# First projections in groups between the token transposes; decay and beta columns split in two parts and multiplied after the tokens; all token loads issued first

## The chip, the cores and the metric

The kernel runs on one core of one Trainium2 chip. The metric is device microseconds of one execution; lower is better. TensorE (PE) does the matrix work, with VectorE (DVE), ScalarE (ACT) and GpSimd (POOL) around it; SyncE (SP), ACT and POOL issue DMAs.

## The reference, cut to what matters

One inference step of a hybrid layer: a combined projection of 1024 prompt tokens and 8 sample tokens, dilated-window attention heads and gated-DeltaNet heads fed from it, an output projection, and a two-level mixture of experts. What the change touches is the start: the projection, the short convolution behind it, and the decay and beta of the DeltaNet heads.

```python
qa, ka, va, ub, zb, ab, bb = split_proj(hp @ w_in[l])
u_ext = jnp.pad(ub, ((0, 0), (CONV_WIDTH - 1, 0), (0, 0)))
q, k, v, g, beta = deltanet_features(short_conv(u_ext, conv_w[l], S), ab, bb, a_log[l], dt_bias[l])
# in deltanet_features:
g = -jnp.exp(a_log) * jax.nn.softplus(a_raw + dt_bias)
beta = jax.nn.sigmoid(b_raw)
# in gated_delta_chunked: gc = cumsum(g) per chunk, decay = exp(gc_i - gc_j),
# then a triangular solve and a scan over chunks
```

## The kernel before, in words

**Tokens.** The 1032 tokens (eight tiles of 128 and one of 8) are loaded as rows into `xt` (L306), odd tiles by SP's queue, even tiles by ACT's. Per tile PE transposes two halves of four 128x128 blocks into a PSUM tile `xps` (L311, pool `tp`, two buffers). DVE copies each half to SBUF as `xf` (L314), ACT rounds it to the high part `xh` (L315, a cast to fp32r), and POOL subtracts the two to get the low part `xl` (L316).

**Decay and beta columns.** The eight columns `wab` of w_in that give decay and beta are multiplied per tile in fp32 with `xf` (L321). The result `ab` holds four partial sums at 32-partition steps; nine matmuls with a selection matrix (L333) add and transpose it into `abt`. From `abt` a chain of small steps on DVE, ACT and PE makes `gdec` (L357), its running sums `gc` (L363, L366), and a transposed copy `gcr` (L379), which goes to DRAM and comes back broadcast as `gb` for each head. The sample tokens' part of `abt` makes a trip through DRAM (`ab_d`, `absm`, L336 to L338) first. `cwr`, the rows of the convolution weights (L386), shares `gcr`'s buffer, so it is loaded when `gcr` has been stored; PE transposes it and the conv state into `cp` (L391), and DVE copies `cw` (L394). No convolution can start before `cw`.

**Projections.** A weight is 128 columns of w_in. `weight` loads it into the single `raw` buffer (L251, SP's queue), ACT casts the high part (L254), DVE subtracts the low part (L255); two buffers `w` hold such pairs. `proj` runs three groups of 344 tokens; a group is 24 matmuls (L278 to L280) into one of two PSUM buffers, and ACT copies the group out. The DeltaNet inputs are called U(j,h) here: j is 0, 1, 2 for the two inputs of `kq` and for `vt`, h the head; their columns start at 1536 + (4j + h) x 128, so w1536 is U(0,0), w2048 U(1,0), w2176 U(1,1), w2688 U(2,1). Two buffers `U` hold a projected input; the next one's first write (a POOL memset, L297) waits for the convolution of the input two before it.

**A head.** DVE convolves (`acc`, L427 to L429, four operations of 1024), ACT takes tanh, DVE makes `kq` (L435); PE multiplies `kk` (L460); DVE applies the decay (`ft`, `qk`, L461, L462); then a substitution of many small DVE steps (`xm`, `xb`, L524 to L534) ends in `xy` (L537), and PE and DVE go on in turns from the `z` of L556. Projections of later inputs stand on PE between these steps.

**Order.** The body is written once; a scheduler sets each engine's order when the program is built, and that order is then fixed: every engine runs its own list from top to bottom, and an instruction whose wait isn't over holds all behind it. `after(later, earlier)` adds edges by hand. `FIRST` names the token tiles behind which the first two weights are split. A DMA waits, besides its data, for the DMA that last used its semaphore (the DMAHW names in the order).

Of the kernel before, what the change touches and what calls it, by code (L numbers as in the profile page):

```python
# [94 lines left out]
def _consts():  # L95
    i = np.arange(P)[:, None]
    j = np.arange(P)[None, :]
    c = [np.eye(P), (i < j), np.broadcast_to(j, (P, P)), i % 64 == np.arange(36)[None, :]]
    cm = np.concatenate([np.asarray(x, np.float32) for x in c], axis=1)

    c = [(i <= j), np.where(j >= i, 0.0, -BIG), i // 16 == j // 16]
    for s in LEVELS:
        c.append((i // (2 * s) == j // (2 * s)) & ((i // s) % 2 == 1) & ((j // s) % 2 == 0))
    c += [i % 16 == np.arange(16)[None, :], i % 32 == np.arange(8)[None, :]]
    cd = np.concatenate([np.asarray(x, np.float32) for x in c], axis=1)
    oh = np.concatenate([_bias_rows(1023 - np.arange(RT)), _bias_rows(DECD)], axis=1)
# [16 lines left out]
def body(ctx, tc, I, O, C):  # L123
    nc = tc.nc
# [8 lines left out]
    dram = pool(ctx, "dram", space=DRAM)  # L133

    cm = const.tile([P, C["c_mats"].shape[1]], F32, name="cm")
    nc.sync.dma_start(out=cm, in_=C["c_mats"])
    ident, strict, iota = (cm[:, n * P:(n + 1) * P] for n in range(3))
    sel36 = cm[:, 3 * P:3 * P + 36]
    ones = const.tile([P, P], F32, name="ones")
# [61 lines left out]
    phs = ExitStack()  # L201
    sm2 = pool(phs, "sm2", bufs=2)
    cd = sm2.tile([P, C["c_delta"].shape[1]], F32, name="cd", bufs=1)
    nc.gpsimd.dma_start(out=cd, in_=C["c_delta"])
    tri, maskb, m16 = (cd[:, n * P:(n + 1) * P] for n in range(3))
    lvl = {s: cd[:, (3 + n) * P:(4 + n) * P] for n, s in enumerate(LEVELS)}
    i16 = cd[:, (3 + len(LEVELS)) * P:][:, :16]
# [19 lines left out]
    def tiles(ap, n=P):  # L227

        return ap[:, 0:S].rearrange("p (a b) -> p a b", b=n)
# [53 lines left out]
            evac(g, ps)  # L283
            yield


    wab = sm2.tile([P, KD, 8], F32, tag="rows", name="wab", bufs=1)
    nc.sync.dma_start(out=wab, in_=I["w_in"][0, :, 3584:3592].rearrange("(k p) c -> p k c", p=P))
    ab = T4("qk", "ab")
    nc.gpsimd.memset(ab, 0.0)  # L290
    xraw, xhi, first = {}, {}, {}

    def conv_in(ct, groups):

# [4 lines left out]
        proj(1536 + ct * P, lambda g, ps: nc.scalar.copy(out=U[:, 3 + g * G:3 + (g + 1) * G], in_=ps), groups)  # L299
        return U  # L300

    for t in range(NT + 1):
        n = P if t < NT else NS
        xt = T4(("ktl", "vh", "zt", "ktl", "vh", "zt", "os", "gb", "ft")[t], f"xt{t}")
        src = I["x_prompt"][0, t * P:(t + 1) * P, :] if t < NT else I["x_sample"][:, 0, :]
        (nc.sync if t % 2 else nc.scalar).dma_start(out=xt[:n], in_=src)  # L306
        xf = tiles(T4(("acc", "vt")[t % 2], f"xf{t}"))
        for b in range(2):
            ps = tps(f"xps{t}_{b}")
            for k in range(4):  # L310
                nc.tensor.transpose(ps[:, k, :n], xt[:n, (4 * b + k) * P:(4 * b + k + 1) * P], ident[:n, :n])  # L311
            hi = xh[:, 4 * b:4 * b + 4, t * P:t * P + n]
            raw_ = xf[:, 4 * b:4 * b + 4, :n]
            xraw[t] = nc.vector.tensor_copy(out=raw_, in_=ps[:, :, :n])  # L314
            xhi[t] = nc.scalar.copy(out=hi, in_=ps[:, :, :n])  # L315
            nc.gpsimd.tensor_tensor(out=xl[:, 4 * b:4 * b + 4, t * P:t * P + n], in0=raw_, in1=hi.bitcast(F32), op=OP.subtract)  # L316
        if t % 4 == 0:
            pab = mm.tile([P, 4, P], F32, tag="mm", name=f"ab_{t}")
        for q in range(2):
            for c in range(4):  # L320
                nc.tensor.matmul(pab[32 * c:32 * c + 8, t % 4, :n], wab[:, 2 * c + q, :], xf[:, 2 * c + q, :n], start=(q == 0), stop=(q == 1))  # L321
        if t % 4 == 3 or t == NT:
            w = (t % 4) * P + n
            for c in range(4):
                r = slice(32 * c, 32 * c + 8)
                (nc.scalar.copy if c in ABA else nc.vector.tensor_copy)(out=ab[r, t // 4 * 512:t // 4 * 512 + w],
                                                                     in_=pab[r].rearrange("p a b -> p (a b)")[:, :w])
# [313 lines left out]
    def biases():  # L641

        rb = small.tile([33, NH], F32, name="rb")
        nc.gpsimd.memset(rb, 1.0)
        nc.gpsimd.dma_start(out=rb[:32], in_=I["rel_bias"])
        cb = T8("dtf", "cb")
        nc.gpsimd.dma_start(out=cb[:33, :RT + 225], in_=C["c_bias"])
        brow = T8("kq", "brow")
        w = RT // 3
        for b in range(3):  # L650
            ps = tps(f"bps{b}").rearrange("p a b -> p (a b)")
            nc.tensor.matmul(ps[:NH, :w], rb, cb[:33, b * w:(b + 1) * w], start=True, stop=True)
# [950 lines left out]
```

## Time and profile before

| | us |
|---|---|
| runs shown | 1529.11, 1530.95, 1539.24 |
| median | 1530.95 |
| profiled execution | 1527.0 |
| its span | 1525.2 |

The profiled execution's own time is 1.8 us above its span, and the median of the runs is 3.95 us above the profiled execution. All times of instructions in this text are of that execution and count from the start of its span. The first 132 us of the span are what the change touches; behind them the fixed orders of before and after are the same on every engine.

### The profile page before, as it was taken

What the parts mean: (1) busy time and instruction counts of PE and PEld (TensorE: products, weight loads), DVE (VectorE), ACT (ScalarE), POOL (GpSimd) and SP (SyncE); (2) the same over time, 40 slices, a digit from 0 to 9 for tenths busy, and PEclk for the clock granted to TensorE, in tenths of its full rate; (3) what the DMA queues carried; (4) which work ended last, traced back from release to release, by engine and by line L of the source; (5) the groups of instructions that cost most, each with busy time, mean ns of one, the idle gap of its engine ahead of it and who ended that gap; (6) DMA issues with size and microseconds to landing.
All of it is one profiled execution on the core that took longest, in us unless ns stands there. A gap on an engine that the chain in (4) does not pass through costs nothing. (4 is left out here: it accounts for less than half of the span.)

```text
span 1525.2 us, 22948 instructions
## 1 busy us (share of the span) xinstructions
PE 1414.8 (93%) x8084; PEld 1168.1 (77%) x8085; DVE 1101.5 (72%) x2105; ACT 881.0 (58%) x1754; POOL 357.4 (23%) x346
## 2 busy tenths in 40 slices
PE   5999999997999989999999969999999999999970
PEld 3989798886987868775767658888888888888850
DVE  4577786867444536356546669999999999999968
ACT  3333534343243424344321149999999999999964
POOL 7020313224022250112301221111112211111115
PEclk9999999999999999995999969999999999999995
DMA  5231110102332461245873569999999999999955
GB/s 173 95 125 29 44 42 24 49 15 75 91 113 84 118 159 55 71 109 174 232 248 132 195 244 349 351 374 372 360 354 352 353 368 368 354 358 367 348 167 222
DMA packets 140016, 309.39 MB, mean 203 GB/s; under 512 B 13483, under 2 KB 71775, under 8 KB 139888
## 3 DMA queue, kind: packets, MB, share of 16 engines
q1 hardware_dynamic: 113928, 259.21, 47.0%
q0 software_dynamic: 14720, 33.92, 8.8%
q10 hardware_dynamic: 11248, 14.75, 3.1%
q8 instruction: 65, 1.06, 0.3%
q14 instruction: 55, 0.45, 0.1%
HBM read 284.04 MB, written 45.24 MB: 216 GB/s over the span
## 5 line engine op out<-in xcount | busy, mean ns | idle before, releaser
L1353 DVE TENSOR_TENSOR wl<-p,wh 128x512 fp32r<-128x512 f32 x436 | 269.9, 682 | 1.1 <-ACT wh L1352 1.1
L1352 ACT CAST wh<-p 128x512 fp32r<-128x512 f32 x436 | 254.1, 633 | 18.3 <-PE h L1389 8.2
L278 PE MATMUL pp<-xh,w 128*128 128x344 f32 x672 | 227.8, 339 | 1.5 <-ACT w L254 1.5
L279 PE MATMUL pp<-xl,w 128*128 128x344 f32 x672 | 221.3, 329 | 0.0
L280 PE MATMUL pp<-xh,w 128*128 128x344 f32 x672 | 220.1, 328 | 0.4 <-DVE w L255 0.4
L1387 PE MATMUL h<-wh,eh 128*128 128x512 f32 x512 | 206.6, 404 | 0.0
L1388 PE MATMUL h<-wl,eh 128*128 128x512 f32 x512 | 205.4, 401 | 0.4 <-DVE wl L1353 0.4
L1389 PE MATMUL h<-wh,el 128*128 128x512 f32 x512 | 201.0, 393 | 0.0
L278 PEld LDWEIGHTS pp<-xh,w 128*128 128x128 f32 x672 | 127.7, 190 | 11.5 <-issue 7.0
L280 PEld LDWEIGHTS pp<-xh,w 128*128 128x128 f32 x672 | 128.0, 190 | 2.3 <-issue 1.2
L279 PEld LDWEIGHTS pp<-xl,w 128*128 128x128 f32 x672 | 128.0, 190 | 1.9 <-issue 1.5
L1359 POOL MEMSET xg<- 128x1024 f32 x32 | 30.5, 953 | 398.2 <-PE xp L1372 396.3
L1388 PEld LDWEIGHTS h<-wl,eh 128*128 128x128 f32 x512 | 96.6, 189 | 25.3 <-DVE wl L1353 7.8
L1353 DVE TENSOR_TENSOR wl_d<-p,wh_d 128x512 fp32r<-128x512 f32 x188 | 115.4, 680 | 0.0
L1352 ACT CAST wh_d<-p 128x512 fp32r<-128x512 f32 x188 | 109.4, 621 | 3.2
L1387 PEld LDWEIGHTS h<-wh,eh 128*128 128x128 f32 x512 | 96.8, 189 | 18.6 <-ACT eh L1374 0.2
L1389 PEld LDWEIGHTS h<-wh,el 128*128 128x128 f32 x512 | 96.4, 188 | 18.6 <-DVE el L1375 0.2
L1428 PE MATMUL py<-wh_d,al 128*128 128x512 f32 x248 | 96.9, 391 | 0.0
L1426 PE MATMUL py<-wh_d,ah 128*128 128x512 f32 x248 | 96.6, 389 | 0.0
L1427 PE MATMUL py<-wl_d,ah 128*128 128x512 f32 x248 | 96.5, 389 | 0.0
L863 ACT ACTIVATE sc<-sc,mx 128x128 f32<-128x128 f32 (+7 forms) x64 | 49.7, 776 | 76.5 <-DVE mx L858 69.8
L1133 PE MATMUL op<-wo,qkm 128*128 128x512 f32 x256 | 84.0, 403 | 0.0
(463 smaller groups left out, 2836.0 us busy)
## 6 DMA issues: line engine op xcount, KB each, us to landing
p<-in_w_up SPq DMA_DIRECT2D x58, 1024.0 KB
p<-in_w_gate SPq DMA_DIRECT2D x51, 1024.0 KB
p<-in_w_down SPq DMA_DIRECT2D x47, 1024.0 KB
rw<-in_w_in SPq DMA_DIRECT2D x28, 512.0 KB
p_vh<-in_w_down SPq DMA_DIRECT2D x12, 512.0 KB
p_ktl<-in_w_gate SPq DMA_DIRECT2D x10, 512.0 KB
p_ktl<-in_w_down SPq DMA_DIRECT2D x10, 512.0 KB
skew_d<-bias_d SPq DMA_DIRECT2D x1, 4608.0 KB
```

Of the source, the lines that this page charges most:

```text
L278: nc.tensor.matmul(ps, wh[:, k, :], xh[:, k, s], start=(k == 0), stop=False)
L279: nc.tensor.matmul(ps, wh[:, k, :], xl[:, k, s], start=False, stop=False)
L280: last[c0, g] = nc.tensor.matmul(ps, wl[:, k, :], xh[:, k, s], start=False, stop=(k == KD - 1))
L1133: mixes[t] = nc.tensor.matmul(pss[b], m[:, k, :], wo[k][:, w, cs[b]], start=(k + i == 0), stop=(k + i == KD + 1))
L1352: nc.scalar.copy(out=wh, in_=src)
L1353: nc.vector.tensor_tensor(out=wl, in0=src, in1=wh.bitcast(F32), op=OP.subtract)
L1387: nc.tensor.matmul(ps, eh[:, k, :], wh, start=(k == 0), stop=False)
L1388: nc.tensor.matmul(ps, eh[:, k, :], wl, start=False, stop=False)
L1389: nc.tensor.matmul(ps, el[:, k, :], wh, start=False, stop=(k == KD - 1))
L1426: nc.tensor.matmul(py[b], ah[:, k, :], wh, start=(k == 0), stop=False)
L1427: nc.tensor.matmul(py[b], ah[:, k, :], wl, start=False, stop=False)
L1428: nc.tensor.matmul(py[b], al[:, k, :], wh, start=False, stop=(k == 3))
```

## The change

- All nine token loads are issued before any transpose, and the first weight's load, w1536, is issued on SP behind the first odd tile's. `wab` and `c_delta` are loaded by ACT's queue, behind the tokens (before: SP's second DMA, and POOL). The matrix table `cm` is loaded in two pieces, its first 128 columns by SP and the others by POOL.
- `xf` is gone: the low part `xl` is DVE's subtraction straight from PSUM; POOL's subtraction is gone.
- `EAGER`: behind token tile 2 stands group 0 of U(0,0); behind tile 5 group 0 of U(1,0) and group 1 of U(0,0); behind tile 8 group 1 of U(1,0). Both groups 2 come where `features` runs.
- The decay and beta columns are split in a high and a low part of 8 columns each, side by side in `whl`, and multiplied with `xh` and `xl` in three groups of 16 matmuls of 344 columns, after the last token tile; one matmul per token tile (K = 16) adds and transposes as before.
- `FIRST` becomes (1, 4): w1536 is split behind tile 1, w2048 behind tile 4. Four more `after` edges hold small operations behind the last tiles.

```diff
-FIRST = (3, 6)
-ABA = (1, 3)
+FIRST = (1, 4)
+EAGER = {2: ((0, 0),), 5: ((4, 0), (0, 1)), 8: ((4, 1),)}
...
-    nc.sync.dma_start(out=cm, in_=C["c_mats"])
+    nc.sync.dma_start(out=cm[:, :P], in_=C["c_mats"][:, :P])
+    nc.gpsimd.dma_start(out=cm[:, P:], in_=C["c_mats"][:, P:])
...
-    nc.gpsimd.dma_start(out=cd, in_=C["c_delta"])
...
-    nc.sync.dma_start(out=wab, in_=I["w_in"][0, :, 3584:3592].rearrange("(k p) c -> p k c", p=P))
     ab = T4("qk", "ab")
-    nc.gpsimd.memset(ab, 0.0)
...
+    xts = []
     for t in range(NT + 1):
         n = P if t < NT else NS
-        xt = T4(("ktl", "vh", "zt", "ktl", "vh", "zt", "os", "gb", "ft")[t], f"xt{t}")
+        xts.append(T4(("ktl", "vh", "zt", "ktl", "vh", "zt", "os", "gb", "ft")[t], f"xt{t}"))
         src = I["x_prompt"][0, t * P:(t + 1) * P, :] if t < NT else I["x_sample"][:, 0, :]
-        (nc.sync if t % 2 else nc.scalar).dma_start(out=xt[:n], in_=src)
-        xf = tiles(T4(("acc", "vt")[t % 2], f"xf{t}"))
+        (nc.sync if t % 2 else nc.scalar).dma_start(out=xts[t][:n], in_=src)
+        if t == 1:
+            parts[U_(0, 0)] = weight(U_(0, 0))
+
+    nc.scalar.dma_start(out=wab, in_=I["w_in"][0, :, 3584:3592].rearrange("(k p) c -> p k c", p=P))
+    nc.scalar.dma_start(out=cd, in_=C["c_delta"])
+    for t in range(NT + 1):
+        n = P if t < NT else NS
+        xt = xts[t]
         for b in range(2):
...
-            raw_ = xf[:, 4 * b:4 * b + 4, :n]
-            xraw[t] = nc.vector.tensor_copy(out=raw_, in_=ps[:, :, :n])
             xhi[t] = nc.scalar.copy(out=hi, in_=ps[:, :, :n])
-            nc.gpsimd.tensor_tensor(out=xl[:, 4 * b:4 * b + 4, t * P:t * P + n], in0=raw_, in1=hi.bitcast(F32), op=OP.subtract)
-        if t % 4 == 0:
-            pab = mm.tile([P, 4, P], F32, tag="mm", name=f"ab_{t}")
-        for q in range(2):
-            for c in range(4):
-                nc.tensor.matmul(pab[32 * c:32 * c + 8, t % 4, :n], wab[:, 2 * c + q, :], xf[:, 2 * c + q, :n], start=(q == 0), stop=(q == 1))
...
+            xlo[t] = nc.vector.tensor_tensor(out=xl[:, 4 * b:4 * b + 4, t * P:t * P + n], in0=ps[:, :, :n], in1=hi.bitcast(F32), op=OP.subtract)
+
+        for ct, g in EAGER.get(t, ()):
+            conv_in(ct, [g])
+
+    whl = r3(T4("z2", "whl")[:, :16 * KD].rearrange("p (k c) -> p k c", c=16))
+    his["ab"] = nc.scalar.copy(out=whl[:, :, 0:8], in_=wab)
+    los["ab"] = nc.vector.tensor_tensor(out=whl[:, :, 8:16], in0=wab, in1=whl[:, :, 0:8].bitcast(F32), op=OP.subtract)
+    for g in range(NG):
+        s = slice(g * G, (g + 1) * G)
+        pab = mm.tile([P, G], F32, tag="mm", name=f"ab_{g}")
+        for k in range(KD):
+            nc.tensor.matmul(pab[:16], whl[:, k, :], xh[:, k, s], start=(k == 0), stop=False)
+            nc.tensor.matmul(pab[:16], whl[:, k, :], xl[:, k, s], start=False, stop=(k == KD - 1))
+        nc.scalar.copy(out=ab[:16, s], in_=pab[:16])
...
-        nc.tensor.matmul(abp[:n, 0, t * 8:(t + 1) * 8], ab[:, t * P:t * P + n], sel8, start=True, stop=True)
+        nc.tensor.matmul(abp[:n, 0, t * 8:(t + 1) * 8], ab[:16, t * P:t * P + n], sel8[:16], start=True, stop=True)
```

How the instructions move is shown at three places. The first is the start of ACT's list, before; DMAHW1 and DMAHW3 are the semaphores of token tiles 0 and 1 there.

```order
L306 DMA xt0_130<-in_x_prompt 128x1024
L306 DMA xt2_185<-in_x_prompt 128x1024
L306 DMA xt4_243<-in_x_prompt 128x1024
L315 ACT_TABLE_LOAD
L315 CAST xh_104<-xps0_0_133 128x4x128 [waits DVE_49]
L315 CAST xh_104<-xps0_1_141 128x4x128 [waits DVE_49]
L306 DMA xt6_298<-in_x_prompt 128x1024 [waits DMAHW1_49]
L315 CAST xh_104<-xps1_0_161 128x4x128 [waits DVE_49]
L315 CAST xh_104<-xps1_1_169 128x4x128 [waits DVE_49]
L306 DMA xt8_356<-in_x_sample 8x1024 [waits DMAHW3_49]
```

The start of ACT's list in the changed kernel; there DMAHW1 is tile 0's load, DMAHW3 tile 2's, and DMAHW4 the load of the first weight w1536.

```order
L304 DMA xt0_128<-in_x_prompt 128x1024
L304 DMA xt2_137<-in_x_prompt 128x1024
L304 DMA xt4_141<-in_x_prompt 128x1024
L304 DMA xt6_145<-in_x_prompt 128x1024
L304 DMA xt8_149<-in_x_sample 8x1024 [waits DMAHW1_49]
L308 DMA wab_126<-in_w_in 128x8x8 [waits DMAHW3_49]
L309 DMA cd_116<-in_c_delta 128x792 [waits DMAHW4_49]
L318 ACT_TABLE_LOAD
L318 CAST xh_105<-xps0_0_153 128x4x128 [waits PE_49]
L318 CAST xh_105<-xps0_1_160 128x4x128 [waits PE_49]
L318 CAST xh_105<-xps1_0_167 128x4x128 [waits PE_49]
L318 CAST xh_105<-xps1_1_174 128x4x128 [waits PE_49]
L254 CAST w1536_134<-rw1536_132 128x1024
```

The table load and the first cast of a token tile stood ahead of the waiting DMA issues and now stand behind three of them.

The second place is PE where `abt` is made, before: the last of the fp32 products of a token tile, the selection matmuls, and the first projection group.

```order
L321 MATMUL ab_8_375<-xf8_358,wab_126 8x8 x5
L333 MATMUL abp_389<-cd_115,ab_128 128x8 [waits PE_49,DMASW4_49,Activation_49,Pool_49]
L333 MATMUL abp_389<-cd_115,ab_128 128x8 x3
L333 MATMUL abp_389<-cd_115,ab_128 128x8 [waits Activation_49]
L333 MATMUL abp_389<-cd_115,ab_128 128x8 x3
L333 MATMUL abp_389<-cd_115,ab_128 8x8 [waits Activation_49]
L278 MATMUL pp1536_0_497<-xh_104,w1536_494 128x344 [waits PE_49]
```

The same place in the changed kernel, with the end of the third `ab` group and, between the selection matmuls, the start of group 2 of U(0,0).

```order
L332 MATMUL ab_2_431<-xh_105,whl_392 16x344
L333 MATMUL ab_2_431<-xl_106,whl_392 16x344
L340 MATMUL abp_450<-cd_116,ab_127 128x8 [waits DMAHW4_49,PE_49]
L340 MATMUL abp_450<-cd_116,ab_127 128x8
L340 MATMUL abp_450<-cd_116,ab_127 128x8 [waits Activation_49]
L340 MATMUL abp_450<-cd_116,ab_127 128x8 x2
L278 MATMUL pp1536_2_551<-xh_105,w1536_134 128x344
L279 MATMUL pp1536_2_551<-xl_106,w1536_134 128x344
L280 MATMUL pp1536_2_551<-xh_105,w1536_134 128x344
L340 MATMUL abp_450<-cd_116,ab_127 128x8 [waits Activation_49]
```

The selection matmuls were the last step of the token phase, ahead of all projections; now they stand behind nine token tiles, four projection groups and the 48 `ab` matmuls.

The third place is DVE at the end of head 0's substitution, before: the split of w2176, the weight of U(1,1), stands inside the substitution.

```order
L533 TENSOR_REDUCE xm0_794<-dt0_684 128x64 [waits DVE_49]
L534 TENSOR_TENSOR xb0_793<-xb0_793,xm0_794 128x8x8 [waits DVE_49]
L524 TENSOR_TENSOR xm0_794<-xy0_717,xb0_793 128x8x7 [waits DVE_49]
L255 TENSOR_TENSOR w2176_1391<-rw2176_1389,w2176_1391 128x1024 [waits DMAHW4_49,PE_49,Activation_49]
L525 TENSOR_TENSOR xb0_793<-xb0_793,xm0_794 128x8x7 [waits DVE_49]
```

The same split in the changed kernel, with the convolution and `kq` of U(0,1) ahead of it.

```order
L544 TENSOR_TENSOR xy0_660<-xb0_736,cd_116 128x1024 [waits DVE_49]
L434 TENSOR_SCALAR acc1_1323<-U1_1234,cw_501 128x1024 [waits Activation_49,Pool_49]
L436 SCALAR_TENSOR_TENSOR acc1_1323<-U1_1234,cw_501,acc1_1323 128x1024 [waits DVE_49] x3
L442 SCALAR_TENSOR_TENSOR kq1_1233<-kq1_1233,acc1_1323 128x1024 [waits DMAHW1_49,Activation_49]
L255 TENSOR_TENSOR w2176_1334<-rw2176_1332,w2176_1334 128x1024 [waits DMAHW5_49,Activation_49]
L255 TENSOR_TENSOR w2688_1430<-rw2688_1428,w2688_1430 128x1024 [waits DMAHW6_49,PE_49,Activation_49]
```

The split moved from inside the substitution to behind `xy`, four convolution operations and `kq`; PE's matmuls of U(1,1) wait for it.

## Rows read from the trace of the kernel before

**Rows 1.** The page, busy time of each engine

```profile
PE 1414.8 (93%) x8084; PEld 1168.1 (77%) x8085; DVE 1101.5 (72%) x2105; ACT 881.0 (58%) x1754; POOL 357.4 (23%) x346
```

**Rows 2.** Windows: busy us of each engine, granted clock, DMA share, GB/s

```profile
core 0: us, PE busy (x) PEld busy (x) DVE busy (x) ACT busy (x) POOL busy (x), PEclk, DMA share, GB/s
0.00:10.00 10.00, 1.94 (x8) 1.58 (x9) 1.60 (x5) 2.46 (x4) 6.63 (x16) 1.00 0.77 238
10.00:12.50 2.50, 1.04 (x16) 0.48 (x16) 0.00 (x0) 0.00 (x0) 0.63 (x1) 1.00 1.02 404
12.50:17.50 5.00, 3.66 (x28) 2.48 (x29) 1.38 (x2) 1.38 (x3) 1.40 (x2) 1.00 1.03 382
41.00:44.00 3.00, 3.00 (x11) 3.00 (x12) 0.44 (x3) 0.23 (x1) 1.12 (x2) 0.50 0.00 0
62.20:71.00 8.80, 8.80 (x58) 8.80 (x57) 6.32 (x14) 5.01 (x8) 0.29 (x2) 1.00 0.33 122
57.50:115.46 57.96, 56.11 (x333) 50.66 (x333) 45.30 (x96) 21.22 (x59) 11.14 (x15) 1.00 0.40 138
365.00:372.50 7.50, 3.55 (x8) 2.01 (x9) 4.82 (x6) 0.91 (x2) 5.42 (x5) 0.54 0.01 3
```

**Rows 3.** Timeline of the token phase: start, us, engine, operation, idle before it

```profile
2.15 1.28 ACT L315 ACT_TABLE_LOAD   x1 [2.02 <-issue]
...
11.25 1.04 PE L321 MATMUL ab<-xf,wab 128*8 128x128 f32 x16 [3.68 <-DMA wab<-in_w_in]
...
16.30 0.53 ACTq L306 DMA_DIRECT2D xt<-in_x_sample  x1
...
17.11 1.10 PE L311 MATMUL xps<-cm,xt 128*128 128x128 f32 x8
...
22.50 1.05 ACT L254 CAST w<-rw 128x1024 fp32r<-128x1024 f32 x1
...
26.48 1.21 DVE L255 TENSOR_TENSOR w<-rw,w 128x1024 fp32r<-128x1024 f32 x1
27.72 1.29 DVE L314 COPY xf<-xps 128x512 f32<-128x512 f32 x2
28.44 1.19 ACT L315 CAST xh<-xps 128x512 fp32r<-128x512 f32 x2 [2.04 <-DVE xf L314]
...
31.26 1.18 ACT L315 CAST xh<-xps 128x512 fp32r<-128x512 f32 x2 [1.63 <-DVE xf L314]
```

**Rows 4.** Timeline, the chain from abt to the convolution weights

```profile
40.98 0.23 DVE L334 COPY abt<-abp 128x64 f32<-128x64 f32 x1 [3.07 <-PE abp L333]
...
46.52 0.19 DVE L343 TENSOR_TENSOR araw<-absm,dtb 128x32 f32<-128x32 f32 x1 [5.08 <-DMA absm<-ab_d]
...
51.15 0.28 DVE L379 COPY gcr<-cps 32x128 f32<-32x128 f32 x1 [0.15 <-PE cps L378]
...
53.70 0.52 POOL L386 DMA_DIRECT2D cwr<-in_conv_w  x1 [1.38 <-DMA gcd<-gcr]
...
57.50 0.20 DVE L394 COPY cw<-cp 128x48 f32<-128x48 f32 x1
```

**Rows 5.** Timeline of DVE and ACT, head 0 to head 1's first convolution

```profile
70.65 0.77 DVE L427 TENSOR_SCALAR acc<-U,cw 128x1024 f32<-128x1024 f32 x1 [2.48 <-ACT U L299]
...
80.09 0.42 DVE L461 TENSOR_TENSOR ft<-kk,dt 128x256 f32<-128x256 f32 x1 [1.35 <-PE kk L460]
...
103.78 0.25 DVE L524 TENSOR_TENSOR xm<-xy,xb 128x56 f32<-128x56 f32 x1
...
109.84 1.23 DVE L255 TENSOR_TENSOR w<-rw,w 128x1024 fp32r<-128x1024 f32 x1 [0.70 <-ACT w L254]
...
115.46 0.75 DVE L427 TENSOR_SCALAR acc<-U,cw 128x1024 f32<-128x1024 f32 x1 [0.21 <-ACT U L299]
...
123.08 1.06 ACT L434 ACTIVATE kq<-acc 128x1024 f32<-128x1024 f32 x1 [2.74 <-DVE acc L429]
```

**Rows 6.** Timeline of PE: first projection, first matmul of U(1,1), first z

```profile
40.88 0.66 PE L278 MATMUL pp<-xh,w 128*128 128x344 f32 x1
...
115.50 0.41 PE L278 MATMUL pp<-xh,w 128*128 128x344 f32 x1
...
131.71 1.03 PE L556 MATMUL z<-cm,xy 128*128 128x128 f32 x8
```

More of the change, by code (lines that the diff above doesn't have):

```diff
@@ L103, in _consts @@
         c.append((i // (2 * s) == j // (2 * s)) & ((i // s) % 2 == 1) & ((j // s) % 2 == 0))
-    c += [i % 16 == np.arange(16)[None, :], i % 32 == np.arange(8)[None, :]]
+    c += [i % 16 == np.arange(16)[None, :], i % 8 == np.arange(8)[None, :]]
     cd = np.concatenate([np.asarray(x, np.float32) for x in c], axis=1)
@@ L287, in body @@
     wab = sm2.tile([P, KD, 8], F32, tag="rows", name="wab", bufs=1)
-    nc.sync.dma_start(out=wab, in_=I["w_in"][0, :, 3584:3592].rearrange("(k p) c -> p k c", p=P))
     ab = T4("qk", "ab")
-    nc.gpsimd.memset(ab, 0.0)
-    xraw, xhi, first = {}, {}, {}
+    xlo, xhi, first = {}, {}, {}
     def conv_in(ct, groups):
@@ L312, in body @@
             hi = xh[:, 4 * b:4 * b + 4, t * P:t * P + n]
-            raw_ = xf[:, 4 * b:4 * b + 4, :n]
-            xraw[t] = nc.vector.tensor_copy(out=raw_, in_=ps[:, :, :n])
             xhi[t] = nc.scalar.copy(out=hi, in_=ps[:, :, :n])
-            nc.gpsimd.tensor_tensor(out=xl[:, 4 * b:4 * b + 4, t * P:t * P + n], in0=raw_, in1=hi.bitcast(F32), op=OP.subtract)
-        if t % 4 == 0:
-            pab = mm.tile([P, 4, P], F32, tag="mm", name=f"ab_{t}")
-        for q in range(2):
-            for c in range(4):
-                nc.tensor.matmul(pab[32 * c:32 * c + 8, t % 4, :n], wab[:, 2 * c + q, :], xf[:, 2 * c + q, :n], start=(q == 0), stop=(q == 1))
[L322 to L327, printed above, removed]
+            xlo[t] = nc.vector.tensor_tensor(out=xl[:, 4 * b:4 * b + 4, t * P:t * P + n], in0=ps[:, :, :n], in1=hi.bitcast(F32), op=OP.subtract)
[11 more added lines that the diff above has]
+        nc.scalar.copy(out=ab[:16, s], in_=pab[:16])
     abt = small.tile([P, NT + 1, 8], F32, name="abt")
@@ L353, in body @@
     ea = small.tile([P, HB], F32, name="ea")
-    nc.scalar.activation(out=ea, in_=alog, func=AF.Exp)
+    exps["a"] = nc.scalar.activation(out=ea, in_=alog, func=AF.Exp)
     nc.scalar.activation(out=sa, in_=sa, func=AF.Ln, bias=1.0)
@@ L657, in biases @@
         rb8 = small.tile([33, NS, NH], F32, name="rb8")
-        nc.vector.tensor_copy(out=rb8, in_=rb[:, None, :].to_broadcast([33, NS, NH]))
+        sums["rb"] = nc.vector.tensor_copy(out=rb8, in_=rb[:, None, :].to_broadcast([33, NS, NH]))
         ps = tps("dbps").rearrange("p a b -> p (a b)")
@@ L1068, in body @@
                 after(i, minima[SUMS[pr][0]][SUMS[pr][1] + n])
+    after(his["ab"], xhi[NT - 1])
+    after(los["ab"], xlo[NT - 1])
+    after(exps["a"], xhi[NT - 1])
+    after(sums["rb"], xlo[NT - 1])
     for n, t in enumerate(FIRST):
         after(his[U_(n, 0)], xhi[t])
-        after(los[U_(n, 0)], xraw[t])
+        after(los[U_(n, 0)], xlo[t])
     for k, (p_, n) in enumerate(WOD):
```

## The prediction

> **What bounds the kernel now.** I read the page's busy times first: PE is busy for 93% of the span [rows 1], so time is won where PE waits or does work that isn't the projection's, and that is the first 41 us: the first projection matmul starts at 40.88 [rows 6]. The timeline of that stretch shows why. A token tile takes 2.82 us (the casts of two tiles start at 28.44 and 31.26, [rows 3]), since DVE's copy, ACT's cast and the next transposes follow each other through two PSUM buffers. From 41 us on I read two things side by side. One is the chain from `abt`: 40.98, sample decay back from DRAM 46.52, `gcr` 51.15, `cwr` issued 53.70, `cw` 57.50 [rows 4]; no convolution starts before its end, so 16.5 us after `abt` is the earliest for DVE's part of head 0. The other is DVE on head 0 and PE's first `z` at 131.71 [rows 5, 6], from where both kernels have the same orders. What the change is worth is how far that `z` moves: everything behind it moves with it, on one core with fixed orders.
>
> **The change, part by part.**
>
> *ACT's list.* Its first cast now stands behind three DMA issues that wait, the last (`c_delta`) for the landing of w1536. When is that? By 10 us the DMAs had moved 2.38 MB, by 12.5 us 3.39 MB, by 17.5 us 5.30 MB at 238, 404 and 382 GB/s [rows 2]. Ahead of or beside w1536 are at least tiles 0 to 2 and itself, four times 0.52 MB, with the tables 2.4 MB: 10 us. Tiles 4 and 6 stand on ACT's queue without a wait; with them it is 3.45 MB, 12.6 us; with all tokens 17.5. Small packets fell behind large ones before: `wab`, 32 KB in pieces of 32 bytes, landed only at 11.25 [rows 3]; w1536's pieces are 512 bytes against 4 KB of the tokens. I take 12.5, with 10 and 16 for the range. Then the issue (0.4 to 0.5) and the table load (1.28) [rows 3], no longer hidden in the wait for the first tile: first cast at 14.2.
>
> *Token tiles.* A half is now four transposes, a cast of 0.59, and DVE's subtraction from PSUM, which no row shows; between 0.65 (the copy of the same 512 from PSUM) and the half of a 1.21 us split, 0.61, there is nothing to choose [rows 3], so 0.65. A tile then takes 2.0 to 2.2 instead of 2.82; POOL's subtraction was no bound and its going is worth nothing. Three tiles (6.1) and the split of w1536 between them (1.2 on DVE) bring group 0's second matmul to 21.5.
>
> *Four early groups.* At the full clock a matmul of 344 columns costs 0.15 to 0.16 (58 in 8.8 us), at half clock 0.27 to 0.29 (11 in 3.0) [rows 2]; 24 cost 3.8 or 6.9. Before, the first projections ran at half clock; I take that for half of this group, 5.1, to 26.6. Tiles 3 to 5 with w2048's split: 3 x 2.0 + 1.2 less overlap, 6.6, to 33.2. 45 matmuls, 7.1, to 40.3. Tiles 6 to 8 under the fourth group: 3.8 of matmuls, 2.9 of transposes, 0.2 of waits, to 47.2.
>
> *The `ab` matmuls.* New: 3 x 16 at 0.157 = 7.5, dense on PE, to 54.7. What goes, the fp32 products of a token tile, lay in PE's waits. The nine selection matmuls, with the copy of the third group to SBUF ahead of the last: 2.1, to 56.8. So `abt` comes at 57.0 against 40.98: **16 us later**. PE has four of six groups done by then, but the chain of [rows 4] is as long as it was, plus 0.7 for the split of U(2,0)'s weight, which DVE does ahead of the sample decay. `cw` comes at about 74.2 against 57.5. Two groups 2 and the first of U(2,0) hide under the chain; then PE stands, since the next input's buffer waits for the first convolution.
>
> *What DVE gets back.* From `cw` on head 0 loses: the wait for U(1,0), 2.48; the wait for `kk`, 1.35, which an operation of the next convolution and a split now fill; two of three splits, 2 x 1.21; the wait in the substitution, 0.70 [rows 5]. That is 6.95. DVE is idle for 12.7 of these 58 us [rows 2], so 8.1 beyond those waits; tanh and the substitution's start keep most of it, and of the rest I take 1.5 as saved, the middle between none and 3: 8.5. `xy`, and the convolution of U(0,1) that starts at 115.46 [rows 5], is then 16.7 - 8.5 = 8.2 later.
>
> *U(1,1).* Before, PE went into it at 115.50, as DVE went into that convolution, since its split had been done at 109.84 [rows 5, 6]. Now its split stands behind four convolution operations (0.75 + 3 x 1.28 = 4.6), tanh (1.06) and ACT's cast (1.05), which stands behind the tanh on ACT: PE starts 6.7 us after where it did. From there to `z` PE has the same matmuls, 16.2 us of them. The first `z` is 8.2 + 6.7 = **14.9 us later**.
>
> The sum: 1527.0 + 14.9 = 1541.9 for the profiled execution, and with the 3.95 that lie between that and the median, **1546 us**, 1.0% slower. Bounds of the terms: w1536's landing -2.5 to +3.5; all early groups at full clock -1.3, or half clock in one more burst +1.5. That is +11 to +20.
>
> **The rivals.**
>
> *PE sets the end (not slower).* If the chain had slack, only PE's work would count. Its six groups, which end at 70.5 [rows 5], of which some 4 us are `cps`, `cp` and bias matmuls that now come later, would end at 64: 2 to 5 us earlier with the landing at 12.5 or 10, 1526 to 1529. For it: 93% busy. Against it: DVE waits 2.48 us for U(1,0) in head 0, and little else there; it runs from `cw` on. It decides if PE has no idle time of its own between 70 and 140 us. Chance 0.14.
>
> *U(1,1) costs nothing.* If `z` were limited elsewhere, 8.2 would remain: 1539. Against it: in the order nothing lies between the split and those matmuls. Chance 0.12.
>
> *Half clock after the new gaps.* PE would idle some 6 us before `kk` and as much before U(1,1). In the trace, 7.5 us in which PE is busy for 3.55 were granted 0.54 [rows 2]: about half of 2.4 GHz. Twelve matmuls at 0.28 instead of 0.157 cost 1.5, 24 cost 2.9, behind each gap: +3 to +5, 1550. The Trainium skill (TensorE: Matmul & The Clock Gate, Part 1) says that the throttled clock is the default and activity releases it, so by that page both gaps would be paid; the row from 365 us agrees, and the row at 41 us, half clock although DVE had just waited 3.07 us for PE's work [rows 4], says that more than idleness lowers it. Chance 0.17.
>
> The forecast itself, with the chain late by 16, has 0.57.
>
> **How the numbers follow.** A measurement of this kernel tells about 1%, 15.3 us, from no change: above 1546.3 is slower. The forecast's own range is 1541 to 1552, cut in about its middle: 0.28 slower, 0.29 same. The half clock falls on the slower side with 0.16 of 0.17; the other two are same, but for 0.02 faster. Together: slower 0.44, same 0.54, faster 0.02. To leave out no more than 2 in 10 the range reaches over the half clock's case with both bounds, 1556, and down to 1529, which takes in the case of 1539 and the upper end of PE's case.
>
> **What would show it.** In the profile of the changed kernel: ACT's first cast at 12 to 16 us and not near 7; the first projection matmul at 19 to 23; `abt` at 54 to 61; `cw` 17 us behind it; PE idle for 5 us or more before `kk` and before U(1,1); the first `z` at 143 to 152; and the same distance from there to the end as before. I am wrong if ACT's first cast isn't held, if w1536 lands with tile 1, or if PE is dense from its first group to `z`.

## The result, and the profile after

| | before | after |
|---|---|---|
| median | 1532.12 (4 runs) | 1556.38 (4 runs, 1551.77 to 1556.9) |
| profiled execution | 1527.0 | 1556.82 |
| its first `z` | 131.71 | 160.73 |

The change makes the kernel 1.4% slower: ratio 1.0143 over the runs, 95% interval 1.0111 to 1.0175 (the two medians alone are 1.6% apart). The forecast was 1546, with a range up to 1556. The direction was right and so were the two late steps, the held cast and the late split; the size was too small: the first `z` came 29.0 us later instead of 14.9, outside the +11 to +20 of the terms' bounds. The rest of the profiled execution is as long as before: 1556.82 - 160.73 = 1396.1 against 1527.0 - 131.71 = 1395.3. The medians are only 24.3 apart because the profiled execution of before is 5.1 under its median, that of after at its median. Of e3, below, one slow execution of 3458 us is left out of the median.

Page of after, busy time of each engine (against [rows 1]):

```profile
PE 1424.6 (92%) x7988; PEld 1175.0 (76%) x7989; DVE 1099.9 (71%) x2100; ACT 879.4 (57%) x1752; POOL 332.6 (21%) x327
```

The shares hardly move, though 29 us are lost: the loss is in the first 161 us. Windows of after, the columns of [rows 2]; the first is the stretch up to the first `z`, the others lie around two stops of PE:

```profile
core 0: us, PE busy (x) PEld busy (x) DVE busy (x) ACT busy (x) POOL busy (x), PEclk, DMA share, GB/s
0.00:160.70 160.70, 121.20 (x662) 104.89 (x664) 77.66 (x151) 49.26 (x112) 22.05 (x44) 0.90 0.30 97
...
84.00:87.40 3.40, 3.34 (x9) 1.55 (x9) 3.04 (x4) 0.25 (x1) 0.00 (x0) 0.50 0.09 13
87.40:92.00 4.60, 0.05 (x1) 0.00 (x0) 4.57 (x11) 2.44 (x4) 0.10 (x1) 0.50 0.45 167
...
93.25:97.40 4.15, 4.14 (x14) 4.15 (x15) 3.40 (x3) 2.32 (x10) 0.10 (x1) 0.50 0.50 206
...
134.77:142.40 7.63, 0.00 (x1) 0.00 (x0) 6.44 (x4) 2.31 (x4) 2.82 (x2) 0.74 0.00 0
142.40:146.80 4.40, 4.37 (x15) 4.14 (x16) 1.28 (x2) 0.00 (x0) 0.00 (x0) 0.50 0.41 110
```

PE is idle for 160.7 - 121.2 = 39.5 us before the first `z`. The same window of the kernel before, up to 131.7, has 19.5:

```profile
0.00:131.70 131.70, 112.20 (x758) 97.52 (x760) 79.63 (x156) 50.53 (x114) 45.42 (x63) 0.97 0.36 118
```

So 20 of the 29 us are idle PE. The other 9 aren't the new columns: with their selection they kept PE busy for 9.9 us, the fp32 products and selection of before for 12.5. They are the projections: the same 456 matmuls into `pp` took 9.6 us longer, with a granted clock of 0.90 instead of 0.97 over the window. Windows of PE for the tile `pp` alone (window, us, PE busy, granted clock, DMA share, GB/s), before and after:

```profile
0.00:131.70 131.70, 77.05 (x456) 0.97 0.36 118
0.00:160.70 160.70, 86.65 (x456) 0.90 0.30 97
```

Timeline of after, the token phase (against [rows 3]): start, us, engine, operation, idle before it and what ended it.

```profile
7.49 0.40 ACTq L308 DMA_DIRECT2D wab<-in_w_in  x1
17.84 0.35 ACTq L309 DMA_DIRECT2D cd<-in_c_delta  x1
18.22 1.28 ACT L318 ACT_TABLE_LOAD   x1 [18.10 <-DMA wab<-in_w_in]
19.52 1.07 ACT L318 CAST xh<-xps 128x512 fp32r<-128x512 f32 x2
...
20.88 1.97 PE L316 MATMUL xps<-cm,xt 128*128 128x128 f32 x8 [13.85 <-DVE xl L319]
...
25.19 0.66 PE L278 MATMUL pp<-xh,w 128*128 128x344 f32 x1
26.33 0.66 PE L279 MATMUL pp<-xl,w 128*128 128x344 f32 x1 [0.48 <-DVE xl L319]
```

Tile 0's transposes end at 7.04, but ACT's list holds the issue of `cd` until 17.84, and tile 0's casts, the PSUM buffers and so PE wait behind it. (The row names `wab` as what ended ACT's wait; in e4, with the same order there, it names `rw`, and in the order of ACT that issue waits for w1536.) Then the chain and head 0 (against [rows 4, 5, 6]):

```profile
61.89 0.22 DVE L341 COPY abt<-abp 128x64 f32<-128x64 f32 x1 [11.18 <-PE abp L340]
...
79.52 0.21 DVE L401 COPY cw<-cp 128x48 f32<-128x48 f32 x1 [4.77 <-PE cp L400]
...
92.00 0.75 DVE L434 TENSOR_SCALAR acc<-U,cw 128x1024 f32<-128x1024 f32 x1
...
123.87 0.26 DVE L531 TENSOR_TENSOR xm<-xy,xb 128x56 f32<-128x56 f32 x1 [3.16 <-ACT xy L519]
...
133.97 0.75 DVE L434 TENSOR_SCALAR acc<-U,cw 128x1024 f32<-128x1024 f32 x1 [0.42 <-POOL xb L526]
134.76 5.44 DVE L436 SCALAR_TENSOR_TENSOR acc<-U,cw,acc 128x1024 f32<-128x1024 f32 x3
...
142.46 1.22 DVE L255 TENSOR_TENSOR w<-rw,w 128x1024 fp32r<-128x1024 f32 x1
```

DVE has all it needs for U(1,0) at 92.00 (no wait, where before it waited 2.48), and PE has nothing to do instead:

```profile
92.02 1.12 PE L487 MATMUL fps<-cm,kq 128*128 128x128 f32 x4 [4.58 <-DVE kq L442]
...
142.43 0.66 PE L278 MATMUL pp<-xh,w 128*128 128x344 f32 x1 [7.66 <-ACT w L254]
...
160.73 1.04 PE L563 MATMUL z<-cm,xy 128*128 128x128 f32 x8
```

### The profile page after: what moved, and what is told of

The parts are those of the page before. It is cut to its first block, busy times and chain, and to the rows that moved or that the text cites. A ratio compares the mean times of both kernels' runs of the same rounds, so it can differ in the third digit from the quotient of the medians.

```text
span 1555.1 us, 22722 instructions
## 1 busy us (share of the span) xinstructions
PE 1424.6 (92%) x7988; PEld 1175.0 (76%) x7989; DVE 1099.9 (71%) x2100; ACT 879.4 (57%) x1752; POOL 332.6 (21%) x327
## 5 line engine op out<-in xcount | busy, mean ns | idle before, releaser
L278 PE MATMUL pp<-xh,w 128*128 128x344 f32 x672 | 230.8, 343 | 8.9 <-ACT w L254 7.7
L280 PE MATMUL pp<-xh,w 128*128 128x344 f32 x672 | 223.1, 332 | 0.3 <-DVE w L255 0.3
L278 PEld LDWEIGHTS pp<-xh,w 128*128 128x128 f32 x672 | 129.9, 193 | 20.0 <-ACT w L254 7.8
L280 PEld LDWEIGHTS pp<-xh,w 128*128 128x128 f32 x672 | 129.9, 193 | 1.8 <-DVE w L255 0.8
## 6 DMA issues: line engine op xcount, KB each, us to landing
p<-in_w_up SPq DMA_DIRECT2D x58, 1024.0 KB, 15.5
p<-in_w_down SPq DMA_DIRECT2D x47, 1024.0 KB, 15.5
p_ktl<-in_w_gate SPq DMA_DIRECT2D x10, 512.0 KB, 10.2
```

Of the source, the lines that this page charges most:

```text
L278: nc.tensor.matmul(ps, wh[:, k, :], xh[:, k, s], start=(k == 0), stop=False)
L280: last[c0, g] = nc.tensor.matmul(ps, wl[:, k, :], xh[:, k, s], start=False, stop=(k == KD - 1))
```

## The experiments

Ratios are to the kernel before, measured on the same chip; `abt`, `cw` and first `z` are read from each profiled execution, PE's idle time from a window up to that `z`.

| run | `abt` | `cw` | first `z` | PE idle | median | ratio (95%) |
|---|---|---|---|---|---|---|
| before | 41.0 | 57.5 | 131.7 | 19.5 | 1532.12 | 1 |
| after | 61.9 | 79.5 | 160.7 | 39.5 | 1556.38 | 1.0143 (1.0111 to 1.0175) |
| e1 | 58.3 | 77.6 | 158.8 | 34.7 | 1552.67 | 1.0131 (1.0093 to 1.0169) |
| e2 | 60.3 | 78.1 | 156.9 | 38.2 | 1554.28 | 1.0149 (1.0117 to 1.0181) |
| e3 | 52.1 | 68.2 | 145.2 | 28.0 | 1540.96 | 1.0062 (1.0040 to 1.0085) |
| e4 | 60.3 | 77.9 | 152.9 | 34.3 | 1548.22 | 1.0106 (1.0073 to 1.0139) |
| e5 | 46.0 | 62.0 | 137.6 | 22.2 | 1534.83 | 1.0028 (1.0011 to 1.0044) |
| e6 | 43.2 | 59.1 | 133.1 | 20.1 | 1530.59 | 0.9997 (0.9983 to 1.0010) |
| e7 | 41.8 | 57.7 | 131.7 | 16.5 | 1527.03 | 0.9987 (0.9972 to 1.0003) |
| e8 | 57.7 | 77.5 | 150.5 | 29.3 | 1548.37 | 1.0104 (1.0077 to 1.0131) |
| e9 | 35.0 | 51.1 | 126.6 | 13.4 | 1522.95 | 0.9946 (0.9928 to 0.9964) |
| e10 | 41.0 | 52.0 | 146.9 | 29.0 | 1546.24 | 1.0090 (1.0072 to 1.0108) |
| e11 | 60.1 | 71.1 | 145.4 | 32.3 | 1542.63 | 1.0063 (1.0040 to 1.0087) |
| e12 | 42.2 | 54.3 | 134.9 | 19.9 | 1531.59 | 1.0006 (0.9992 to 1.0020) |

**e1, the two issues off ACT.**

```diff
-    nc.scalar.dma_start(out=wab, ...)
-    nc.scalar.dma_start(out=cd, in_=C["c_delta"])
+    nc.gpsimd.dma_start(out=wab, ...)
+    nc.gpsimd.dma_start(out=cd, in_=C["c_delta"])
```

> The changed kernel with the loads of wab and c_delta issued on POOL; ACT has only the token loads ahead of its first cast. Theory of the chain (what delays abt delays the first z by as much): ACT's first cast near 7 us instead of 19.52; w1536 still lands near 17.8, so its cast and split end near 20.5 and the first group's second matmul comes at 20.5 to 21.5 instead of 26.33; abt and the first z 5 us earlier (57 and 156), time 1551. Rival, the token tiles' landing sets the first group, not ACT's hold: second matmul stays within 1 us of 26.3, time 1556. Rival, PE sets the end: abt moves but z doesn't, time 1555 to 1557.

The first cast came at 7.20. But the wait only moved: ACT's cast of w1536 is the next that needs the landing, and tile 2's casts stand behind it. Timeline of ACT in e1:

```profile
18.45 1.05 ACT L254 CAST w<-rw 128x1024 fp32r<-128x1024 f32 x1 [7.08 <-DMA rw<-in_w_in]
19.40 1.07 ACT L318 CAST xh<-xps 128x512 fp32r<-128x512 f32 x2
```

Timeline of PE in e1, the first group of projections:

```profile
8.81 1.94 PE L316 MATMUL xps<-cm,xt 128*128 128x128 f32 x8 [1.41 <-DMA xt<-in_x_prompt]
...
21.41 0.65 PE L279 MATMUL pp<-xl,w 128*128 128x344 f32 x1 [0.72 <-DVE xl L319]
21.86 0.49 PE L280 MATMUL pp<-xh,w 128*128 128x344 f32 x1
22.15 0.49 PE L278 MATMUL pp<-xh,w 128*128 128x344 f32 x1
```

The second matmul came 4.9 us earlier, as the chain theory said; then the group ran at 0.286 us a matmul until 27.2 and `abt` gained 3.6, `z` 1.9. By its time alone e1 can't be told from the changed kernel.

**e2, w1536 ahead of all of SP's tokens** (its `weight` call stands before the token loop).

> As e1_issues_on_pool, and w1536's load is issued on SP ahead of all of SP's token tiles. Theory of the chain: w1536 lands at 7 to 11, the first group is set by tile 2's arrival, second matmul at 14 to 18, abt 50 to 54, first z 149 to 153, time 1544 to 1548. Rival, 512-byte pieces always fall behind the tokens' 4 KB pieces whatever the place in SP's queue: landing 16 to 18, as in e1, time 1551. Rival, PE sets the end: abt earlier, z not, 1555 to 1557.

The rival on the landing held: issued at 1.21, w1536 still wasn't done at 17, since the issue of SP's last tile waited 12.0 us for it, up to 17.3. Tile 1, now behind it on SP's queue, reached PE at 18.70 instead of the 8.81 of e1. Waits of SP's queue (total us, times, longest) and timeline of PE in e2:

```profile
SPq L305 <- DMA rw<-in_w_in: 12.0, 1, 12.0
...
18.70 1.94 PE L315 MATMUL xps<-cm,xt 128*128 128x128 f32 x8 [11.50 <-DMA xt<-in_x_prompt]
```

Its place in the queue doesn't make this load early; it makes late what stands behind it.

**e3, no early groups.**

```diff
-EAGER = {2: ((0, 0),), 5: ((4, 0), (0, 1)), 8: ((4, 1),)}
+EAGER = {}
```

> The changed kernel with EAGER empty: all six projection groups behind the tokens and the ab matmuls, as in the kernel before; the loads, the low parts and the split decay and beta columns stay. Theory of the chain: first cast still 19.5, tile 8 done near 38, abt at 47 to 52 instead of 61.89, cw 17 us behind it; DVE waits 2 to 4 us for U(1,0) again; first z 8 to 10 us earlier (151 to 153), time 1546 to 1549. Rival, PE's own work sets the end, so that early groups pay: PE's six groups end 5 us or more later than 76, z stays or comes later, time 1556 to 1562.

The chain theory held, and more than held: `abt` 9.8 us earlier, `z` 15.5, the time 5 us under what I had given. What goes beyond `abt`, 5.7 us, is order, as I read it: without early groups the scheduler puts the split of w2176 back into the substitution, as in the kernel before. The next run takes that edge alone.

**e4, the split first.**

```diff
+    after(convs[1], los[U_(1, 1)])   # convs[1]: the first operation of U(0,1)'s convolution
```

> The changed kernel with one edge: DVE's split of w2176 stands ahead of the convolution of U(0,1) instead of behind it. Theory of the forecast's last term: PE goes into U(1,1) 5 to 7 us earlier (135.5 to 137.5 instead of 142.43) and the first z as much earlier, 154 to 156, time 1549 to 1551. Rival, U(1,1) costs nothing: z within 1 us of 160.7, time 1555 to 1557.

Timeline of PE in e4, the first matmuls of U(1,1):

```profile
134.43 0.42 PE L278 MATMUL pp<-xh,w 128*128 128x344 f32 x1 [1.29 <-ACT w L254]
...
136.48 0.42 PE L280 MATMUL pp<-xh,w 128*128 128x344 f32 x1 [1.15 <-DVE w L255]
```

PE's stop of 7.66 is down to 1.29 and 1.15, and `z` is 7.8 earlier; 1.6 of that is an earlier `abt`, since the first group ran at the full clock in this execution. So the edge itself is worth 6.2 us at `z`; the medians are 8.2 apart, the ratios 0.4%, about 6 us.

**e5 and e6, the token phase without holds.** e5 joins e1 and e3; e6 also places the columns' matmuls among the tiles:

```diff
+        if t in (3, 6, 8):
+            columns((3, 6, 8).index(t))   # 16 matmuls of one group of 344 tokens, and its copy to ab
```

> EAGER empty, as in e3_no_early_groups, and the loads of wab and c_delta on POOL, as in e1_issues_on_pool. First cast at 7.2; ACT's cast of w1536, which lands near 17.8, stands behind tile 1 and holds tile 2's cast until 19.4, against 24.15 in e3. Theory of the chain: abt 47 to 48 instead of 52.1, first z near 141 instead of 145.2, time 1537 to 1540. Rival, half clock: PE falls to the lower clock in the hold and gives the gain back in the transposes and the ab matmuls, abt 50 to 52, time 1541 to 1543.

> As e5_no_early_pool, and the ab matmuls stand in three groups of 16 behind tiles 3, 6 and 8 instead of all 48 behind tile 8. Theory of the chain: only 16 of them remain between the last tile and abt, abt 3 to 5 us earlier than in e5 (43 to 45), z as much, time 1534 to 1537. Rival, the 32 matmuls among the tiles delay the tiles by as much as they save behind them: abt and time as in e5.

Both went the way of the chain theory and a little further: `abt` 46.0 and 43.2, `z` 137.6 and 133.1. Against e1, e5 shows the early groups, with the order of the splits that goes with them: 12.3 us at `abt`, 21.2 at `z`, 17.8 in time. e6 is as fast as the kernel before.

**e7, w1536 behind the tokens**, with the splits behind tiles 3 and 6 again.

> As e6_columns_in_place, and w1536's load is issued on SP behind the token tiles, its split behind tile 3 and w2048's behind tile 6 (as in the kernel before). Theory of the chain: no hold on ACT any more, tile 8 done at 28 to 31, abt at 35 to 38, ahead of the 40.98 of the kernel before; first z 126 to 130, time 1525 to 1530, as fast as the kernel before or up to 6 us faster. Rival, PE sets the end once the chain is early: abt 35 to 38 but DVE waits for U(1,0) by what was gained, first z 130 to 134, time 1530 to 1534.

I expected tile 8 at 28 to 31; its last cast came at 34.8. The hold had only moved once more, timeline of ACT in e7:

```profile
22.06 1.04 ACT L254 CAST w<-rw 128x1024 fp32r<-128x1024 f32 x1 [5.45 <-DMA rw<-in_w_in]
```

With `abt` 0.8 later than before, `z` stands at 131.7, where it stood.

**e8, the early groups in the best setting for them** (e1, e4 and the columns in place).

> The changed kernel with its four early groups kept; wab and c_delta on POOL (e1), the ab matmuls behind tiles 3, 6 and 8 ahead of the early groups there, and DVE's split of w2176 ahead of the convolution of U(0,1) (e4). Theory of the chain: the early groups delay tile 8 and so abt, which is the 58.3 of e1 less one group of 3.8, 54 to 55; first z 158.8 - 7.8 - 3.8, 146 to 148; time 1541 to 1545, slower than e6. Rival, early groups pay once they don't delay the columns' matmuls: time at or below e6_columns_in_place.

They don't pay: 1548.37, 17.8 us over e6, with the split early in both; this is the cleanest price of the early groups. `abt` came at 57.7, later than the 54 to 55 I gave, and the time 3 us above my range: what delays `abt`, I think, is PE's whole work ahead of tile 8, and the columns' matmuls are part of that wherever they stand.

**e9, the splits behind the landing.** As e7, with one line:

```diff
-FIRST = (3, 6)
+FIRST = (6, 8)
```

> As e7_weight_behind, but w1536's split stands behind tile 6 and w2048's behind tile 8, so that ACT doesn't wait for w1536's landing (at 22.0 in e7, where it held tile 4's casts for 5.5 us). Theory: tile 8 done 4 to 6 us earlier than in e7 (29 to 31 instead of 35), abt at 36 to 38 instead of 41.8 and PE's dense stretch as much earlier; first z at 126 to 128 instead of 131.7; time 1521 to 1524. Rival, PE: the first projections then run at half clock for longer, or wait for w2048, and first z stays within 2 us of e7: 1525 to 1529.

It beats both kernels: 0.9946 of the kernel before, some 8 us. Timeline of DVE in e9 at `abt` and at the convolution of U(1,0):

```profile
35.01 0.22 DVE L343 COPY abt<-abp 128x64 f32<-128x64 f32 x1 [3.08 <-PE abp L342]
...
63.61 0.75 DVE L436 TENSOR_SCALAR acc<-U,cw 128x1024 f32<-128x1024 f32 x1 [1.65 <-ACT U L296]
```

`abt` is 6.0 us earlier than before, `z` 5.1: here the projections start earlier too, at 27.33 instead of 40.88, so PE and the chain move together.

**e10, e11, e12: only the chain shorter.** The prompt tokens' decay no longer waits for the sample tokens' trip through DRAM, in the kernel before (e10) and the changed one (e11):

```diff
+    softplus(slice(0, NT))        # araw, sa, gdec of the prompt: on to gc, gcr, cw
...
+    softplus(slice(NT, NW))       # of the samples, behind cw
```

> The kernel before, with the prompt tokens' decay computed ahead of the sample tokens' trip through DRAM, so that the chain from abt to cw is 4 to 5 us shorter, with abt itself and the projections as they were. If the chain alone sets the first z in the kernel before: cw at 52.5 to 54, first z 127 to 128, time 4 us under the kernel before. Rival, PE is as late as the chain there: PE is dense from 40.9 to 100, U(1,0) is still done at 70.5, DVE waits for it 6 to 7 us instead of 2.48, and first z stays within 1 us of 131.7, time within 2 us.

> The changed kernel with the same edit as e10: the chain from abt to cw 4 to 5 us shorter, abt as it was at 61.9. Theory of the chain: PE has idle time behind its six groups, so cw comes at 75 instead of 79.5 and the first z 4 to 5 us earlier, 156 to 157, time 1551 to 1552. Rival, PE sets the end in the changed kernel: z and time stay within 1 us and 2 us.

e10 answers something else than I asked. `cw` came 5.5 earlier, but the scheduler moved other things with it: the bias matmuls ahead of U(0,0)'s last group, and the split of w3072 from inside U(1,0)'s convolution to behind it. Timeline of DVE in e10:

```profile
61.89 0.75 DVE L435 TENSOR_SCALAR acc<-U,cw 128x1024 f32<-128x1024 f32 x1 [5.04 <-ACT U L299]
...
106.49 1.23 DVE L255 TENSOR_TENSOR w<-rw,w 128x1024 fp32r<-128x1024 f32 x1 [5.44 <-ACT w L254]
```

Windows of e10, the stretch ahead of that split, columns as in [rows 2], and timeline of PE behind it:

```profile
90.00:100.00 10.00, 0.94 (x5) 0.51 (x5) 8.45 (x16) 4.38 (x20) 1.60 (x3) 0.60 0.35 107
...
100.15 4.84 PE L519 MATMUL fb<-dt,cd 128*128 128x480 f32 x6 [7.99 <-DVE dt L517]
```

PE is busy for 0.94 of 10 us there: it waits for DVE's `dt`, and the projections of the late weight, which could have filled that wait, stand behind it. In e11 `z` moved by 15.3 where I gave 4 to 5: the chain from `abt` to `cw` is 6.6 shorter and `abt` was 1.8 earlier, and the split of w2176 stands in the substitution again, the edge of e4, worth 6.2 there. So e12 repeats e10 with the lists put back:

```diff
+    after(bps_[0], last[U_(0, 0), 2])
+    after(convs[4, 2], los[3072])
```

> As e10_before_prompt_decay_first, with two edges that put back what e10's order had moved: the bias matmuls behind U(0,0)'s last group, and the split of w3072 inside the convolution of U(1,0), as in the kernel before. If the chain alone sets the first z in the kernel before: cw near 52, DVE's convolutions as much earlier, first z at 127 to 128, time about 4 us under the kernel before. If PE is as late as the chain there: DVE waits for U(0,0) or U(1,0) by what cw gained, the convolution of U(1,0) still starts within 1.5 us of 70.65, first z within 2 us of 131.7, time within 3 us of the kernel before.

Timeline of DVE in e12, `cw` and the two convolutions of `kq`:

```profile
54.31 0.21 DVE L396 COPY cw<-cp 128x48 f32<-128x48 f32 x1 [2.04 <-PE cp L395]
58.44 0.75 DVE L435 TENSOR_SCALAR acc<-U,cw 128x1024 f32<-128x1024 f32 x1 [3.43 <-POOL us L430]
...
72.54 0.77 DVE L435 TENSOR_SCALAR acc<-U,cw 128x1024 f32<-128x1024 f32 x1 [3.71 <-ACT U L299]
```

`abt` was 1.2 late, `cw` still 3.2 early; DVE then waits for U(0,0) (the wait ends with POOL's small copy `us` of it) and again for U(1,0), and the time is that of the kernel before. The first `z`, at 134.9, missed my 2 us by one, and the convolution of U(1,0), at 72.54, my 1.5 by 0.4; of the 3.2 us at `z`, 2.0 beyond the later `abt` stay unexplained. In the kernel before, PE is as late as the chain.

## Why the prediction was right in kind and too small

Of the prediction's signs, the distance from `abt` to `cw`, the stop before U(1,1) (7.66 us) and the distance from `z` to the end came as given. The first cast (19.5 for 12 to 16), the first projection (25.2 for 19 to 23), `abt` (61.9 for 54 to 61), the stop before `kk` (4.58 for 5 or more) and `z` (160.7 for 143 to 152) didn't. That the time ends at the upper end of the range is in part luck: 1556 was drawn for the half clock with both bounds, and two other terms filled it; and the profiled execution of after stood 0.4 over its median where I had added 3.95 to it.

*ACT's list.* Right in kind: the issue of `c_delta` holds the first cast. Mis-sized: w1536 landed at 17.8, not 12.5, and above my 16. I had counted bytes; e2 shows that ahead of SP's tokens this load is as slow. That is the +4.9 by which `abt` (20.9 later) missed my 16: from the landing on, tiles, groups, the 7.5 for the columns and the selection together took what they were given, within 0.4 us.

*The chain.* 17.6 us from `abt` to `cw` against 17.2 forecast.

*What DVE gets back* failed: 8.5 forecast, 22.0 - 18.5 = 3.5 measured. Two of the three splits are gone, as forecast, and so are the waits that I had named (for U(1,0), for `kk`, the 0.70). But DVE's idle time from `cw` to the convolution of U(0,1) fell only from 12.7 us [rows 2] to 54.45 - 44.21 = 10.2, by 2.4, where my terms asked for 6.0. Windows of after, columns as in [rows 2], and timeline of PE and DVE:

```profile
79.52:133.97 54.45, 47.55 (x232) 39.62 (x231) 44.21 (x93) 17.71 (x54) 10.25 (x15) 0.81 0.32 117
...
81.10 2.73 PE L659 MATMUL bps<-cb,rb 33*8 33x384 f32 x4
...
82.58 0.55 DVE L660 COPY brow<-bps 8x384 f32<-8x384 f32 x1 [1.12 <-PE bps L659]
```

New waits came: 1.85 for the bias matmuls (`bps`) against 0.6 before, 0.70 for U(2,0) and 0.9 for `ktl`; and 3.16 for `xy` stands where 3.02 for ACT's `z` had stood. Four bias matmuls took 2.73 us instead of 1.45: the granted clock was 0.61 to 0.50 there (80 to 84 us), and 1.00 before. Besides, `xy`'s first operation took 2.32 instead of 1.22, beside POOL. I had looked for waits that end, and priced what PE and POOL would make DVE wait for at nothing.

*U(1,1).* Forecast 6.7, measured 26.9 - 18.5 = 8.4: the convolution took 1.6 longer, one of its operations 2.80 instead of 1.28 beside POOL. e4 confirms the term in kind by taking it away.

*Half clock.* I made it a rival, with 0.17; it came with the forecast's mechanism, and not only behind the two stops. Around the stop of 4.58 us the granted clock was 0.50, that is 1.2 GHz, from 82 us on, while PE was still busy (3.34 of 3.40 us in 84.0 to 87.4), through the stop and up to 97.4; in the 2 us from 78 to 80, before it fell, PE had been busy for 1.15. In the stop of 7.66 us it fell again to 0.50, and from 114 to 118 it was 0.57. About 14, 21 and 11 matmuls took 0.286 instead of 0.157: 1.8, 2.7 and 1.4 us. The two that I had priced come to the 3 to 5 that I gave, but what shows on the way to `z` is 2.1 from U(1,1)'s start on (18.30 against 16.21) and the 1.3 that the bias matmuls cost DVE, counted above.

The misses add up: 4.9 + 0.4 + 5.0 + 1.7 + 2.1 = 14.1, which is 29.0 - 14.9.

*PE sets the end* is refuted for the changed kernel: PE's idle time rose by 20 us, and e11 moved `z` by 15.3 with a shorter chain, of which the split's edge, by e4, explains only some 6. For the kernel before it is half true: in e12 the chain alone brought nothing there. A later chain costs about what it is late (e5: `abt` 5.0, `z` 5.9; e6: 2.2 and 1.4); an earlier one paid in e9, where PE's projections started earlier too.

What stays open: how much of e3's and e11's gain belongs to the order of the splits, beyond what e4 shows; no run kept the late split with a shorter chain. The cause of the slow landing wasn't isolated either.

## What to carry to other kernels

Where one engine's dense work and a chain of small steps end together, filling the engine's gaps with work that isn't due yet delays the chain, and the gaps come back behind it: put the chain's own matmuls into the gaps and let the projections wait. A load that is issued early isn't there early, and each instruction that needs it in order (an issue, a cast, a split) holds everything behind it on its engine; place these behind the landing that the trace shows: from e7 to e9 that one line brought 5.1 us at `z`. An edit that moves one step can move splits and bias work in the scheduler's order, so compare the lists before believing the time.

## What the runs showed of the hardware that I had not expected

*A load's time among others.* View of the DMA issues of after: queue, count, KB, median us to landing.

```profile
rw<-in_w_in SPq DMA_DIRECT2D x28, 512.0 KB, 3.9
...
xt<-in_x_prompt ACTq DMA_DIRECT2D x4, 512.0 KB, 9.0
xt<-in_x_prompt SPq DMA_DIRECT2D x4, 512.0 KB, 16.3
```

The weight loads take 3.9 us in the median; w1536 took 16 beside the tokens, and 13 in e7, issued at 8.89 behind them. In after the rate was 155 GB/s from 7.5 to 10 us at a DMA share of 0.82, against 408 from 5 to 7.5. The Trainium skill (DMA: Bandwidth & Descriptors, Queues, rings and completion order) says that each DMA engine takes turns between the queues packet by packet. If a turn moves fewer bytes where the pieces are small, a queue with small pieces gets less. The landings agree with that: SP's tokens, three of four behind w1536, took 16.3 us in the median, ACT's 9.0. No run varied the piece size.

*The clock after a stop.* The lists of after and e4 are the same up to the first group, and so is PE's stop ahead of tile 1 (13.85 and 13.36 us). The group's matmuls ran at 0.286 us in after and at 0.157 in e4, with a granted clock of 1.00 recorded for both. So a stop alone doesn't tell the pace behind it, and the record of the clock didn't show this one.

*DVE beside POOL.* Timeline of after, two places where both work on 1024 columns:

```profile
104.76 2.39 POOL L505 TENSOR_TENSOR kq<-kq,gb 128x1024 f32<-128x1024 f32 x1 [4.82 <-PE kk L467]
105.92 2.32 DVE L474 TENSOR_TENSOR xy<-ft,cd 128x1024 f32<-128x1024 f32 x1
...
135.07 2.72 POOL L555 TENSOR_TENSOR vh<-vh,nk 128x1024 f32<-128x1024 f32 x1 [0.96 <-ACT vh L554]
136.07 2.80 DVE L436 SCALAR_TENSOR_TENSOR acc<-U,cw,acc 128x1024 f32<-128x1024 f32 x1
```

`xy` ran beside POOL's `kq` for its first 1.23 us and took 2.32 instead of the 1.22 of before. The second of U(0,1)'s convolution operations ran beside POOL's `vh` for 1.72 us and took 2.80 instead of 1.28; `vh` itself had started within the first, and took 2.72 instead of the 1.90 of e4, where it started first. The Trainium skill (SBUF — State Buffer, SBUF: two separate sides) says that of a DVE operation with two inputs in SBUF and a POOL operation, the one that starts first holds their shared ports for its whole instruction and the other waits. The trace agrees: the later one lost 1.1 and 1.5 us of the 1.23 and 1.72 that it stood beside the earlier. DVE's `ft` and `qk`, which read PE's product `kk`, ran beside the same `kq` and took 0.41 each, as before.
